# Hybrid attention encoder on one core: superblocks walked back and forth, keys of the next head group made for the current superblock, maxima taken through DRAM

## The chip, the cores and the metric

The kernel runs on one NeuronCore of a Trainium2 chip. TensorE (PE) multiplies, VectorE (DVE) and ScalarE (ACT) work elementwise, GpSimd (POOL) does small elementwise work, SyncE (SP) issues every DMA of this kernel. The metric is device time in microseconds, from one launch.

## The reference, cut to what matters

One layer is applied to two requests with the same weights: a prompt of 2048 rows and a sample of 512 rows, 1024 wide.

```python
h = rmsnorm(x, g_pre) * (1.0 + scale) + shift        # scale, shift, gate from silu(c) @ w_ada + b_ada
qa, ka, va, ga, qb, kb, vb, gb = split(h @ w_in)
# A: 8 heads of 64, three dilated windows (128,1), (512,4), (2048,16), mixed by their softmax denominators
ya = dilated_mixture(rope(qa), rope(ka), va) * silu(ga)
# B: 4 heads of 2 x 64 queries and keys, 128 values, dense over all rows
a  = softmax(q1 @ k1.T / 8) - lam * softmax(q2 @ k2.T / 8)
yb = rmsnorm(a @ v, g_sub) * (1.0 - lam_init) * silu(gb)
y  = concat(ya, yb) @ w_out
out = x + gate * rmsnorm(y, g_post)
```

## The kernel before

**Tiles.** A superblock is 512 rows of a request: the prompt has four (here p0 to p3), the sample one (s). The heads are cut into eight groups of 128 columns each of queries, gates, keys and values; groups 4 to 7 are dense attention (B), groups 0 to 3 dilated attention (A), and they are worked in the order 4, 0, 5, 1, 6, 2, 7, 3, so B and A alternate. Every f16 operand is held as a high and a low half, and a projection is three products (L433), so that the result has nearly f32 precision.

**Stages.** The first part, ahead of the group loop, makes the modulation, the normalised input h of each superblock (`first_h`, `make_h`), spills h to DRAM (`spill_h`, 2 MB for a superblock) and projects the first group. Then comes a double loop, group by group and superblock by superblock (L1036 to L1092), 40 stages in all. A stage's main work is the attention of one superblock in one group: 4 items of 128 queries in B, 8 items (2 heads by 4 blocks) in A. Its filler, woven between, is projection work for later stages: `qg_proj` of the next superblock (L523: queries, transposed by DMA into the tile Qc at L550, then 24 products for the gate), and `kv_proj` of the *next* superblock for the *next* group (L448). In the fifth stage the filler is both projections of p0 for the next group. The next stage's first scores (L602 in B, L711 in A) read Qc.

**h.** Two buffers in SBUF hold h of two superblocks (`HB`). `load_h` (L368) brings one back from DRAM as four DMAs of 512 KB; it is called once before the loop and then at the start of nearly every stage, 39 times.

**What sets the order.** The program is recorded with `interleave` (L963), which lets the filler run as far as the main work has come, against costs noted in the code, and with `LEAD` all zero. A scheduler then orders each engine's instructions by its own estimate of when they can run; each engine runs its list in order. In the group loop PSUM holds three buffers of scores, one of projections (`pj`) and one of outputs (`pv`, L1034).

**Maxima over all partitions.** Every weight group is scaled by a power of two from its largest element. `raw_scale` (L286) and `wo_scale` (L823) take it for w_in and w_out, `y_scale` (L874) for each superblock's y. All call `allmax`: a PE transpose of one column into a `pv` buffer, a DVE maximum over 128 numbers, and a PE product that spreads it to all partitions:

```python
tp = PT([P, 512], tag)
nc.tensor.transpose(tp[0:1, 0:P], col, id_sb)        # L178
m = T(tn, [1, 1], F32, "am1")
V.reduce_max(m, tp[0:1, 0:P], axis=AX.X)             # L180
bc = PT([P, 512], tag)
mm(bc[:, 0:1], lhsT=one_sb, rhs=m, start=True, stop=True)   # L182
```

**Output projection.** `out_proj` (L898) makes 20 tiles of 128 rows, 48 products each (L918), in part as filler of the last group, the rest after it. A tile begins with `y_first` (L885), which loads y from DRAM, and for a superblock's first tile calls `y_scale` before that.

Of the kernel before, what the change touches and what calls it, by code (L numbers as in the profile page):

```python
# [29 lines left out]
AQ = 1  # L30
LEAD = [0, 0, 0, 0]
OPC = [0, 20, 24, 24, 30]
# [5 lines left out]
def hybrid_kernel(ctx, tc, x_p, x_s, w_in, w_ada, w_out, cvec, cols, lamv, gsub,  # L38
# [136 lines left out]
    def allmax(col, tag="pv"):  # L175
# [7 lines left out]
        return bc[:, 0:1]  # L183

    RAW = {}

# [99 lines left out]
    def raw_scale(n):  # L286

        g, raw = ORDER[n], RAW[n]
        mg = T(tn, [P, 8], F32, "mg")
        for q in range(KT):  # L290
            V.tensor_reduce(mg[:, q:q + 1], raw[:, q, :], axis=AX.X, op=ALU.max, apply_absolute_value=True)
            yield 0.0
        ag = T(tn, [P, 1], F32, "ag")
        V.reduce_max(ag, mg, axis=AX.X)
        E = T(tn, [P, 1], F32, "E")
        S = C([P, 1], F32, f"wS{g}")
        pow2(E, S, allmax(ag), f"w{g}")
        smul(isw[:, g:g + 1], E, 2.0 ** -13)
        smul(S, S, 2.0 ** 12)
        WS[n] = S  # L300
        yield 0.0
# [107 lines left out]

    def first_h(r):  # L410

        for _ in norm_x(r, 0):
            pass
        xs = XN[r, 0]
        xT = [T(kv, [P, 4, 512], F32, "V") for _ in range(2)]
# [7 lines left out]
        hT = T(big, [P, 2, KT, 512], F16, "h", bufs=HB)  # L423
        HT[r, 0] = hT
        for k in range(KT):
# [3 lines left out]
            V.tensor_sub(hT[:, 1, k, :], xk, hT[:, 0, k, :])  # L429
        spill_h(r, 0)  # L430
        yield
# [391 lines left out]
    def wo_scale():  # L823
# [12 lines left out]
        wo["i"] = C([P, 1], F32, "woi")  # L836
        pow2(E, wo["S"], allmax(ag), "wo")
        smul(wo["i"], E, 2.0 ** -13 * 2.0 ** -13)
# [35 lines left out]
    def y_scale(r, c):  # L874

        ag = T(tn, [P, 1], F32, "ag")
        V.reduce_max(ag, yam[:, c + (r == "s") * NSB["p"], :], axis=AX.X)
        s = T(tn, [P, 4], F32, "ys")
        pow2(s[:, 0:1], s[:, 1:2], allmax(ag), "y")
        V.tensor_scalar(s[:, 0:1], s[:, 0:1], wo["i"], None, op0=ALU.mult)  # L880
        smul(s[:, 1:2], s[:, 1:2], 2.0 ** 12)
        V.tensor_scalar(s[:, 2:3], s[:, 0:1], s[:, 0:1], 1.0 / D, op0=ALU.mult, op1=ALU.mult)
        YS[r, c] = s

    def y_first(r, c, j):  # L885

        if j == 0:
            y_scale(r, c)
        s = YS[r, c]
# [92 lines left out]
    NS = len(SBS)  # L982
    outp = out_proj([(r, c, j) for r, c in SBS for j in range(4)])

# [10 lines left out]
    g0 = ORDER[0]  # L995
    h0 = first_h("p")
    next(h0)
# [19 lines left out]
    raw_load(1)  # L1017
    prev = ("p", 0)
    for n, (r, c) in enumerate(SBS):
        work = [kv_proj(r, g0, c)]  # L1020
        if n == 0:
            work.append(qg_proj(r, g0, c))
        if n == 2:
# [3 lines left out]
        if n + 1 < NS:  # L1027
            interleave(make_h(*SBS[n + 1]), 6.4, chain(*work), 11 * len(work))
        else:
            run(chain(*work))  # L1030
    if g0 < 4:
        load_v1("p", g0, 0)
    load_h(*SBS[1])
    psum(1024, 3, 1, 1)  # L1034

    for n, g in enumerate(ORDER):  # L1036
        if n + 1 == NU and g < 4:
            psum(1024, 2, 3, 1)
        g2 = ORDER[n + 1] if n + 1 < NU else None
        for i, (r, c) in enumerate(SBS):  # L1040
            fl, fc = [], 0.01
            side = iter(())
            if n + 1 < NU or i + 2 < NS:
                load_h(*SBS[(i + 2) % NS])
            if i == 0 and n + 2 < NU:
# [8 lines left out]
            elif n + 2 == NU:  # L1054
                if i < 2:
                    side = gate_half(i)
                elif i == 2:
                    side = wo_scale()
                elif i == 3:
                    side = load_wo(0)  # L1060
            elif i == 0:
                side = chain(load_wo(1), call(load_gg))
            if i == 0:
                at_n[3] = 0
            if i == 0 and g2 is not None:
                for x in "ps":
                    new_unit(x, g2)
            r2, c2 = SBS[(i + 1) % NS]
            if i + 1 < NS:
                fl.append(qg_proj(r2, g, c2))  # L1070
                fc += 11
                if g < 4:
                    fl.append(call(load_v1, r2, g, c2))
            if g2 is not None:
                fl.append(kv_proj(r2, g2, c2))
                fc += 11
                if i + 1 == NS:
                    for x in "ps":
                        fl.insert(0, call(unit_scalars, x, g2))
                    fl.append(qg_proj(r2, g2, c2))  # L1080
                    fc += 11
                    if g2 < 4:
                        fl.append(call(load_v1, r2, g2, c2))
            if g2 is None and i >= 1:
# [99 lines left out]
```

## Time and profile before

| what | us |
|---|---|
| median of 3 runs | 2179.29 |
| lowest, highest | 2177.16, 2189.58 |
| profiled execution | 2191.28 |
| its span, first to last instruction | 2189.5 |
| PE busy in the span | 1910.8 |
| DVE busy in the span | 1541.1 |
| ACT busy in the span | 1152.7 |

The profile is one execution, and its own time is 12.0 us above the median. A busy PE in it is the union of its matmuls. SyncE's work is DMA issues, which the page does not count as busy; each issue has a duration in the trace all the same.

### The profile page before, as it was taken

To read this page: it belongs to the slowest core of one execution; us is meant where nothing else is said; L and a number is where in the kernel's file an instruction comes from. 1 tells how busy PE (TensorE), PEld (TensorE's weight loads), DVE (VectorE), ACT (ScalarE), POOL (GpSimd) and SP (SyncE) were. 2 spreads that over 40 slices of the span, in tenths; PEclk is the share of its full clock that TensorE was granted. 3 is DMA by queue.
4 is the path that set the end of the run, shared out by engine and by line. 5 is a ranking of instruction groups with operands and counts; after the bars stand their busy time and mean duration, and the time that the engine had idled before them with its cause. 6 is when DMAs were issued, how large, how long until landed. Compare 5 with 4: busy or idle time off the path is not lost. (4 is left out here: it accounts for less than half of the span.)

```text
span 2189.5 us, 47689 instructions
## 1 busy us (share of the span) xinstructions
PE 1910.8 (87%) x18545; PEld 1285.2 (59%) x18545; DVE 1541.1 (70%) x3428; ACT 1152.7 (53%) x2278; POOL 394.9 (18%) x1049
## 2 busy tenths in 40 slices
PE   4878997898989988888899888897989878989898
PEld 2665665666767666666566666574665554444443
DVE  3777998676669988666599886666888665455543
ACT  3555665555547666555467665554566644333321
POOL 0122222221112222111122221111222121100000
PEclk7789999999999999999999999898999888999999
DMA  7585787888857789898477888888776779665553
GB/s 293 171 253 126 138 163 149 188 158 165 186 130 152 145 196 188 140 173 192 114 151 145 184 188 155 170 183 235 147 148 157 159 163 191 122 133 126 130 163 111
DMA packets 726834, 360.12 MB, mean 164 GB/s; under 512 B 639808, under 2 KB 686672, under 8 KB 723152
## 3 DMA queue, kind: packets, MB, share of 16 engines
q1 hardware_dynamic: 726608, 357.08, 73.6%
q8 instruction: 145, 2.38, 0.5%
q14 instruction: 81, 0.66, 0.1%
HBM read 164.79 MB, written 36.97 MB: 92 GB/s over the span
## 5 line engine op out<-in xcount | busy, mean ns | idle before, releaser
L460 PE MATMUL pj<-w,h 128*128 128x256 f16 x3840 | 480.9, 281 | 29.1 <-DVE V L476 8.2
L460 PEld LDWEIGHTS <-h 128*128 128x128 f16 x3840 | 379.1, 101 | 103.9 <-issue 40.5
L618 ACT ACTIVATE pp<-sc,nb 128x1024 f32<-128x1024 f32 (+1 forms) x288 | 304.3, 1060 | 100.2 <-DVE sc L611 83.2
L534 PE MATMUL pj<-w,h 128*128 128x128 f16 x3840 | 257.1, 223 | 15.0 <-ACT q L541 8.5
L534 PEld LDWEIGHTS <-h 128*128 128x128 f16 x3840 | 231.6, 100 | 43.4 <-issue 32.5
L557 PE MATMUL pj<-h,w 128*128 128x512 f16 x960 | 230.7, 392 | 17.9 <-ACT q L541 17.9
L656 PE MATMUL pv<-V,at 128*128 128x128 f16 x3072 | 207.5, 227 | 38.1 <-DVE yt L681 29.0
L656 PEld LDWEIGHTS <-at 128*128 128x128 f16 x3264 | 201.9, 102 | 64.6 <-issue 47.8
L747 DVE SCALAR_TENSOR_TENSOR hl<-pp,Z,hl 128x640 f16<-128x640 f32 (+2 forms) x160 | 140.3, 881 | 119.4 <-DMA at<-hl 71.6
L443 POOL TENSOR_TENSOR rp<-q,tab_sb 128x64 f32<-128x64 f32 x160 | 67.3, 420 | 788.4 <-ACT q L466 469.5
L745 ACT ACTIVATE hl<-pp,Z 128x640 f16<-128x640 f32 (+2 forms) x160 | 130.3, 823 | 132.5 <-DMA at<-hl 108.7
L611 DVE TENSOR_SCALAR_CACHE_REDUCE sc<-sc,us,nb 128x1024 f32<-128x1024 f32 x128 | 172.3, 1346 | 37.1 <-PE sc L608 15.9
L611 DVE TENSOR_SCALAR_CACHE_REDUCE sc<-sc,us 128x1024 f32<-128x1024 f32 (+1 forms) x160 | 188.1, 1179 | 10.8 <-PE sc L608 10.2
L636 ACT ACTIVATE hl<-pp,rz 128x1024 f16<-128x1024 f32 (+1 forms) x144 | 155.6, 1095 | 60.7 <-issue 38.7
L731 ACT ACTIVATE pp<-pp,nb 128x640 f32<-128x640 f32 (+2 forms) x160 | 131.5, 822 | 105.9 <-DVE nb L726 100.1
L644 DVE SCALAR_TENSOR_TENSOR hl<-pp,rz,hl 128x1024 f16<-128x1024 f32 (+1 forms) x144 | 174.5, 1223 | 16.8 <-DMA at<-hl 5.9
L602 PE MATMUL sc<-K,Qc 128*128 128x512 f16 x512 | 158.6, 389 | 30.2 <-ACT pp L618 29.5
L557 PEld LDWEIGHTS <-w 128*128 128x128 f16 x960 | 94.1, 100 | 135.6 <-issue 42.0
L634 DVE SCALAR_TENSOR_TENSOR pp<-pp,rz,pp 128x1024 f32<-128x1024 f32 (+1 forms) x144 | 171.2, 1225 | 1.9
L918 PEld LDWEIGHTS <-w 128*128 128x128 f16 x960 | 92.9, 99 | 125.0 <-issue 17.0
L711 PE MATMUL sc<-K,Qc 128*32 128x512 f16 (+1 forms) x1024 | 119.2, 371 | 27.0 <-DMA Qc<-tq 17.1
L724 DVE CUSTOM_DVE_ANT_0 pp<-sc,maskp,us 128x384 f32<-128x384 f32 (+1 forms) x128 | 85.8, 678 | 71.0 <-PE sc L717 70.8
(200 smaller groups left out, 2843.9 us busy)
## 6 DMA issues: line engine op xcount, KB each, us to landing
h<-hp SPq DMA_DIRECT2D x124, 512.0 KB, 6.0
pp<-in_x_p_dram SPq DMA_DIRECT2D x32, 512.0 KB, 5.0
raw<-in_w_in_dram SPq DMA_DIRECT2D x8, 2048.0 KB, 8.1
h<-hs SPq DMA_DIRECT2D x32, 512.0 KB, 5.7
out_dram<-pp SPq DMA_DIRECT2D x20, 512.0 KB, 2.9
at<-hl SPq DMA_TRANSPOSE x608, 3.2
hp<-h SPq DMA_DIRECT2D x4, 2048.0 KB, 9.3
yp<-yt SPq DMA_DIRECT2D x32, 256.0 KB, 3.2
```

The lines of the kernel that those rows point to most:

```text
L460: mm(ps[:, jj, :], lhsT=hT[:, a, k, j * P:(j + 1) * P], rhs=w[:, k, b, :], start=(k == 0 and i == 0), stop=(k == KT - 1 and i == 2))
L534: mm(ps[:, jj, 0:128], lhsT=hT[:, a, k, j * P:(j + 1) * P], rhs=w[:, k, b, 0:128], start=(k == 0 and i == 0), stop=(k == KT - 1 and i == 2))
L557: mm(ps, lhsT=w[:, k, b, 128:256], rhs=hT[:, a, k, :], start=(k == 0 and i == 0), stop=(k == KT - 1 and i == 2))
L602: mm(ps[:, n * 512:(n + 1) * 512], lhsT=Qc[:, j, m, 0, :], rhs=K[:, t:t + 4, m, :], start=True, stop=False)
L611: V.tensor_scalar(ps[:, :HW], ps[:, :HW], u["nsc"], nb[:, 0:1] if hf else 3e38, op0=ALU.mult, op1=ALU.min, accum_out=nb[:, hf:hf + 1])
L618: act(pt[m, hf][:, :HW], pss[hf][:, :HW], AF.Exp, scale=-1.0, bias=nb[:, NH - 1:NH], accum_out=Z[:, 2 * m + hf:2 * m + hf + 1])
L634: V.scalar_tensor_tensor(a, a, rz[:, 2:3], pt[0, hf][:, :HW], op0=ALU.mult, op1=ALU.add)
L636: act(hi[:, :HW], a, AF.Copy, scale=rz[:, 3:4])
L644: V.scalar_tensor_tensor(lo[:, :HW], a, sg, hi, op0=ALU.mult, op1=ALU.subtract)
L656: mm(po[:, :128], lhsT=a[:, k, :], rhs=Vv[:, k, 128 * b:128 * b + 128], start=(k == 0 and i == 0), stop=(k == NT - 1 and i == 2))
L731: act(sb[:, :NA], sb[:, :NA], AF.Exp, scale=-1.0, bias=nb[:, 1:2], accum_out=Z[:, 0:1])
L747: V.scalar_tensor_tensor(lo[:, :NA], sb[:, :NA], rz, hi[:, :NA], op0=ALU.mult, op1=ALU.subtract)
```

## The change

1. The sample's superblock goes to the middle: p0, p1, s, p2, p3. Groups at even places of the order walk that list forwards, those at odd places backwards, so a group begins with the superblock on which the one before ended.
2. The filler of a stage is now `kv_proj` of the *current* superblock for the next group, then `load_h` of the superblock two places on (if the group has one), then `load_v1` and `qg_proj` of the next superblock. In a group's last stage, `qg_proj` is of the same superblock for the next group. `load_h` is called 24 times.
3. Before the loop h is made from p3 to p0, and the first `qg_proj` stands at the end instead of beside the second superblock's `make_h`.
4. `LEAD` is replaced by a lead of 0.1 of the main work's cost.
5. All later maxima (`raw_scale` from the second group on, `wo_scale`, `y_scale`), 13 in number, go through `allmax_slow`: write the column to DRAM, read it back to every partition, DVE maximum over 128 numbers in each.
6. `y_scale` is called as soon as the eighth group's y of a superblock is written (in `y_out`), not when its first output tile begins. `gate_half`, `wo_scale` and the first `load_wo` are one stage later.

```diff
+    def allmax_slow(col):
+        d = dr.tile([P, 1], F32, tag=nm("amd"), name=nm("amd"))
+        nc.sync.dma_start(d, col)
+        row = T(tn, [P, P], F32, "amr", bufs=2)
+        nc.sync.dma_start(row, d.rearrange("p o -> (p o)").partition_broadcast(P))
+        m = T(tn, [P, 1], F32, "amc", bufs=2)
+        V.reduce_max(m, row, axis=AX.X)
+        return m
...
-        pow2(E, S, allmax(ag), f"w{g}")
+        pow2(E, S, (allmax if n == 0 else allmax_slow)(ag), f"w{g}")
...
         y_made[r, c] = y_made.get((r, c), 0) + 1
+        if y_made[r, c] == NU:
+            y_scale(r, c)
...
+    SBS.insert(NSB["p"] // 2, SBS.pop())
+    WAY = [SBS[::1 - 2 * (n % 2)] for n in range(NU)]
+    outp = out_proj([(r, c, j) for r, c in WAY[-1] for j in range(4)])
...
-            if n + 1 < NU or i + 2 < NS:
-                load_h(*SBS[(i + 2) % NS])
...
-            r2, c2 = SBS[(i + 1) % NS]
-            if i + 1 < NS:
-                fl.append(qg_proj(r2, g, c2))
-                fc += 11
-                if g < 4:
-                    fl.append(call(load_v1, r2, g, c2))
-            if g2 is not None:
-                fl.append(kv_proj(r2, g2, c2))
+            if g2 is not None:
+                fl.append(kv_proj(r, g2, c))
                 fc += 11
+            if i + 2 < NS:
+                fl.append(call(load_h, *way[i + 2]))
+            r2, c2, gq = (*way[i + 1], g) if i + 1 < NS else (r, c, g2)
+            if gq is not None:
...
+                if gq < 4:
+                    fl.append(call(load_v1, r2, gq, c2))
+                fl.append(qg_proj(r2, gq, c2))
                 fc += 11
...
-            interleave(main, mc, weave(chain(*fl), side), fc, LEAD[2 * (r == "p") + (g < 4)])
+            interleave(main, mc, weave(chain(*fl), side), fc, -AHEAD * mc)
```

What the scheduler made of it shows at three places. In the rows below weight loads and repeats are left out; the numbers behind names only keep buffers apart. Lines of the changed kernel are 10 to 12 higher: its L544, L567, L614, L620, L668, L723, L777 are L534, L557, L602, L608, L656, L711, L765 of before.

PE, the second group (A), where the dense group before it ends. Before: the last queries of p0 (`pj_5252`, 20 products without a break), 24 gate products, the first scores with its Qc.

```order
L656 MATMUL pv_5086<-Vs_454,at 128x128
...
L534 MATMUL pj_5252<-w_1573,h_3974 128x128
...
L557 MATMUL pj_5328<-h_3974,w_1573 128x512
...
L677 MATMUL pv_5164<-id_sb,o_5129 128x128
...
L711 MATMUL sc_5372<-K_1782,Qc_5111 32x384
```

The same place in the changed kernel, where the group begins with p3: last queries (`pj_5181`), 48 value products, scores of the dense group's last item, gate, scores.

```order
L544 MATMUL pj_5181<-w_1420,h_3479 128x128
...
L668 MATMUL pv_4812<-V_443,at 128x128
...
L620 MATMUL sc_4937<-K_442,Qc_4314 128x512
...
L567 MATMUL pj_5243<-h_3479,w_1420 128x512
...
L614 MATMUL sc_5104<-K_442,Qc_4314 128x512
...
L723 MATMUL sc_5277<-K_1772,Qc_5090 32x384
```

Between the last query product and the first score that reads it stood the gate alone; now 48 value products and 16 score products stand there too.

PE, the fourth group (A), at the start of a middle stage. Before, p3 to s: behind the 24 gate products (`pj_14368`) 32 score products of p3 stand ahead of the first that reads the new Qc (`Qc_14167`).

```order
L557 MATMUL pj_14368<-h_13501,w_7969 128x512
...
L711 MATMUL sc_14670<-K_8586,Qc_13515 32x384
...
L717 MATMUL sc_14670<-K_8586,Qc_13515 32x256
...
L711 MATMUL sc_14713<-K_8586,Qc_13515 32x384
...
L717 MATMUL sc_14713<-K_8586,Qc_13515 32x256
...
L711 MATMUL sc_14793<-Ks_8590,Qc_14167 32x128
```

The changed kernel, p3 to p2: behind the last query (`pj_12444`) and the 24 gate products (`pj_12557`) stands one value product, then the first score with the new Qc (`Qc_12353`).

```order
L544 MATMUL pj_12444<-w_7902,h_9833 128x128
...
L567 MATMUL pj_12557<-h_9833,w_7902 128x512
...
L777 MATMUL pv_12915<-at,V_8543 128x128
...
L723 MATMUL sc_12806<-K_8540,Qc_12353 32x512
```

What stood between the gate and the new scores is gone there.

The weight maximum in the second group. Before, on PE in the third group's p1 stage: transpose, key and value products, scores, spreading product.

```order
L608 MATMUL sc_9777<-K_5368,Qc_8602 128x512
L178 MATMUL pv_9675<-id_sb,ag_9671 1x128
...
L460 MATMUL pj_9979<-w_6687,h_8579 128x256
...
L608 MATMUL sc_9783<-K_5368,Qc_8602 128x512
L182 MATMUL pv_9679<-am_1475_9677,one_sb 128x1
```

The same maximum in the changed kernel, on SP: `amd` is the DRAM column, `amr` its copy in every partition.

```order
L761 DMA_TRANSPOSE at<-hl_8194 128x5x128
L188 DMA amd_9462<-ag_9458 128x1
L494 DMA_TRANSPOSE K_5273<-tk_8150 128x4x128
L583 DMA yp_117<-yt_7796 128x512
L190 DMA amr_9464<-amd_9462 128x128
L760 DMA_TRANSPOSE at<-hl_8247 128x5x128
```

Both PE instructions are gone; SP's list has two more issues, the second of which reads what the first wrote.

## Rows read from the trace of the kernel before

**Rows 1.** The page: busy time and share by engine, and 40 slices.
```profile
PE 1910.8 (87%) x18545; PEld 1285.2 (59%) x18545; DVE 1541.1 (70%) x3428; ACT 1152.7 (53%) x2278; POOL 394.9 (18%) x1049
PEclk7789999999999999999999999898999888999999
```

**Rows 2.** Windows (length; PE, PEld, DVE, ACT, POOL busy; clock): start, groups 3, 4, 7.
```profile
0.00:171.30 171.30, 123.06 (x917) 93.64 (x918) 99.52 (x260) 80.31 (x146) 31.47 (x81) 0.81 0.69 236
...
629.10:866.60 237.50, 218.26 (x2167) 150.21 (x2168) 210.84 (x362) 152.70 (x302) 57.79 (x146) 0.98 0.78 163
866.60:1070.40 203.80, 174.48 (x2153) 130.58 (x2153) 129.79 (x408) 106.14 (x215) 31.51 (x98) 0.95 0.82 162
...
1508.00:1790.20 282.20, 238.39 (x2227) 160.36 (x2227) 225.98 (x393) 164.00 (x324) 61.77 (x153) 0.92 0.76 167
```

**Rows 3.** SP's issues by line: duration ns (min/median/max), first and last start.
```profile
L748 SPq DMA_TRANSPOSE at<-hl x160: 1177/1234/3210, 441.1 to 2072.1; - x160
L550 SPq DMA_TRANSPOSE Qc<-tq x80: 1231/1254/2327, 91.7 to 1971.0; - x80
L371 SPq DMA_DIRECT2D h<-hp x124: 326/430/2009, 151.2 to 1827.3; - x124
```

**Rows 4.** PE's waits: who for whom, us in total, times, longest.
```profile
PE sc L711 <- DMA Qc<-tq: 24.1, 12, 5.0
...
PE pv L178 <- DVE ag L294: 10.6, 2, 9.6
...
PE pv L178 <- DVE yt L780: 4.4, 2, 2.4
...
PE pj L534 <- DMA h<-hp: 3.1, 1, 3.1
PE pv L182 <- DVE am L180: 3.0, 3, 1.4
PE pv L178 <- DVE ag L877: 3.0, 1, 3.0
```

**Rows 5.** Timeline of PE around the first output tile (start, length, idle before).
```profile
1844.76 0.37 PE L178 MATMUL pv<-id_sb,ag 128*1 128x128 f32 x1 [2.98 <-DVE ag L877]
...
1855.66 1.03 PE L918 MATMUL pj<-raw,w 128*128 128x512 f16 x2 [6.07 <-ACT w L894]
```

**Rows 6.** Window over the same place.
```profile
1841.80:1858.50 16.70, 6.48 (x42) 2.66 (x43) 9.60 (x26) 5.45 (x8) 0.00 (x0) 0.59 1.06 232
```

**Rows 7.** DMA issues: count, KB each, us to landing.
```profile
h<-hp SPq DMA_DIRECT2D x124, 512.0 KB, 6.0
...
h<-hs SPq DMA_DIRECT2D x32, 512.0 KB, 5.7
...
V<-vbp SPq DMA_DIRECT2D x64, 80.0 KB, 2.5
...
gg<-hl SPq DMA_DIRECT2D x1, 8.0 KB, 1.3
```

**Rows 8.** Windows of last stages (s): fourth, third and seventh group.
```profile
1010.70:1070.40 59.70, 47.38 (x554) 37.12 (x545) 34.18 (x111) 25.92 (x56) 7.90 (x28) 0.91 0.74 152
...
838.00:866.60 28.60, 23.77 (x240) 15.55 (x241) 18.66 (x42) 14.11 (x34) 8.18 (x22) 0.88 0.95 177
...
1743.60:1790.20 46.60, 30.91 (x317) 23.90 (x317) 30.99 (x73) 25.07 (x59) 13.36 (x33) 0.89 0.72 147
```

**Rows 9.** Timeline of PE where the seventh group ends.
```profile
1790.16 1.68 PE L711 MATMUL sc<-K,Qc 128*32 128x384 f16 x10 [5.01 <-DMA Qc<-tq]
```

**Rows 10.** Timeline of PE, fourth group, p3 to s.
```profile
1004.64 5.35 PE L557 MATMUL pj<-h,w 128*128 128x512 f16 x24
...
1014.07 0.29 PE L711 MATMUL sc<-Ks,Qc 128*32 128x128 f16 x6 [3.05 <-DMA Qc<-tq]
```

**Rows 11.** Timeline of SP over the same stretch.
```profile
1007.35 1.23 SPq L748 DMA_TRANSPOSE at<-hl  x1
1008.67 1.23 SPq L749 DMA_TRANSPOSE at<-hl  x1
1010.00 1.26 SPq L550 DMA_TRANSPOSE Qc<-tq  x1
```

**Rows 12.** Timeline of ACT there: the copy of the last queries, then L547.
```profile
1003.55 0.38 ACT L541 ACTIVATE q<-pj 128x256 f32<-128x256 f32 x1
...
1005.19 0.63 ACT L547 ACTIVATE tq<-q 128x512 f16<-128x512 f32 x1 [0.15 <-POOL q L446]
```

More of the change, by code (lines that the diff above doesn't have):

```diff
@@ L30 @@
 AQ = 1
-LEAD = [0, 0, 0, 0]
+AHEAD = 0.1
 OPC = [0, 20, 24, 24, 30]
@@ L408, in make_h, with first_h @@
         spill_h(r, c)
-    def first_h(r):
-        for _ in norm_x(r, 0):
+    def first_h(r, c):
+        for _ in norm_x(r, c):
             pass
-        xs = XN[r, 0]
+        xs = XN[r, c]
         xT = [T(kv, [P, 4, 512], F32, "V") for _ in range(2)]
@@ L423, in first_h @@
         hT = T(big, [P, 2, KT, 512], F16, "h", bufs=HB)
-        HT[r, 0] = hT
+        HT[r, c] = hT
         for k in range(KT):
@@ L429, in first_h @@
             V.tensor_sub(hT[:, 1, k, :], xk, hT[:, 0, k, :])
-        spill_h(r, 0)
+        spill_h(r, c)
         yield
@@ L877, in y_scale @@
         V.reduce_max(ag, yam[:, c + (r == "s") * NSB["p"], :], axis=AX.X)
-        s = T(tn, [P, 4], F32, "ys")
-        pow2(s[:, 0:1], s[:, 1:2], allmax(ag), "y")
+        s = T(tn, [P, 4], F32, "ys", bufs=5)
+        pow2(s[:, 0:1], s[:, 1:2], allmax_slow(ag), "y")
         V.tensor_scalar(s[:, 0:1], s[:, 0:1], wo["i"], None, op0=ALU.mult)
@@ L982, in hybrid_kernel @@
     NS = len(SBS)
-    outp = out_proj([(r, c, j) for r, c in SBS for j in range(4)])
+    SBS.insert(NSB["p"] // 2, SBS.pop())
+    WAY = [SBS[::1 - 2 * (n % 2)] for n in range(NU)]
+    outp = out_proj([(r, c, j) for r, c in WAY[-1] for j in range(4)])
     def upto(gen, cost):
@@ L995, in hybrid_kernel @@
     g0 = ORDER[0]
-    h0 = first_h("p")
+    h0 = first_h(*SBS[-1])
     next(h0)
@@ L1017, in hybrid_kernel @@
     raw_load(1)
-    prev = ("p", 0)
-    for n, (r, c) in enumerate(SBS):
+    for n, (r, c) in enumerate(SBS[::-1]):
         work = [kv_proj(r, g0, c)]
-        if n == 0:
-            work.append(qg_proj(r, g0, c))
         if n == 2:
@@ L1027, in hybrid_kernel @@
         if n + 1 < NS:
-            interleave(make_h(*SBS[n + 1]), 6.4, chain(*work), 11 * len(work))
+            interleave(make_h(*SBS[-2 - n]), 6.4, chain(*work), 11 * len(work))
         else:
-            run(chain(*work))
+            run(chain(*work, qg_proj(r, g0, c)))
     if g0 < 4:
-        load_v1("p", g0, 0)
-    load_h(*SBS[1])
+        load_v1(*SBS[0][:1], g0, SBS[0][1])
     psum(1024, 3, 1, 1)
@@ L1039, in hybrid_kernel @@
         g2 = ORDER[n + 1] if n + 1 < NU else None
-        for i, (r, c) in enumerate(SBS):
+        way = WAY[n]
+        for i, (r, c) in enumerate(way):
             fl, fc = [], 0.01
             side = iter(())
-            if n + 1 < NU or i + 2 < NS:
-                load_h(*SBS[(i + 2) % NS])
             if i == 0 and n + 2 < NU:
@@ L1054, in hybrid_kernel @@
             elif n + 2 == NU:
-                if i < 2:
-                    side = gate_half(i)
-                elif i == 2:
+                if 1 <= i < 3:
+                    side = gate_half(i - 1)
+                elif i == 3:
                     side = wo_scale()
-                elif i == 3:
+                elif i == 4:
                     side = load_wo(0)
```

12 lines of the change are left out of this document (3 added, 9 removed).

## The prediction

> **What bounds the kernel now.** I read the page first: PE is busy 87% of the span, far above the others, and its granted clock is below full in most slices [rows 1]. So PE's own work is the floor, and what can be won is PE's idle time (2189.5 - 1910.8 = 279 us) and what the lower clock adds. The change removes almost no PE work, so the question is which of PE's waits go and which come.
>
> Then the windows by stage of the program [rows 2]. The start is the worst stretch: 48 us idle of 171, clock 0.81. A dense group (the third) has PE idle 19 us of 237.5, with DVE busy 211: there PE and DVE are both near their limit. A dilated group (the fourth) has PE idle 29 us of 203.8 with DVE at 130, so DVE is not its limit. One transposing issue holds SP 1.23 us, whatever its tile [rows 3]. A dilated group issues 80 of them for its weights (4 and 1 superblocks of 8 items, high and low), 10 for its queries and 10 for the next group's keys: 100 x 1.23 = 123 us of SP, before plain DMAs. SP's list is therefore long in the very groups in which PE idles most, and a transfer that PE needs stands behind others there. Last, PE's waits by cause [rows 4]: the largest that this change can touch is the one for Qc, 24.1 us in 12 times, all in dilated groups.
>
> **Part by part.** The sum is made against the profiled execution, 2191.3 us.
>
> *Maxima off PE.* 13 of 16 go. The waits in front of L178 and L182 are 10.6 + 4.4 + 3.0 + 3.0 us [rows 4], but 9.6 of the first is one wait, which I take as that of the first weight group, which keeps its maximum on PE. 11.4 us go. Around the first output tile PE also stands 6.07 us for the tile's scaled y, behind that chain [rows 5]; with the scale made earlier I take half of it, 3 us. That stretch of 16.7 us has a clock of 0.59 and 6.5 us of PE work [rows 6]; at full clock about half of that work's time is saved, 3 us. Gain: 17 us.
>
> *The price of the way through DRAM.* Two issues and the landing of the first, for which SP must wait before it issues the second, with everything behind it in its list held: weight transposes, Qc, the next h. The trace has no such pair. The nearest single rows: a small write to DRAM lands 1.3 us after issue, an 80 KB load after 2.5 [rows 7]. SP held: between 0 (the order puts other ready issues between the two) and 13 x 2.5 = 33 us. In the order shown two issues stand between them, in others none. I take 1.3 us in four of the thirteen, 5 us: the write is nearest in size to the one added, and the weight groups' maxima fall in dense stages as often as in dilated ones. The DVE maximum (128 numbers in every partition) I cost at nothing, since results are wanted a stage later; in the last group it has the remaining output tiles as cover.
>
> The Trainium skill, page "DMA: Bandwidth & Descriptors", section "Two DMAs through the same engine are not ordered", says that a DMA which reads what another wrote must be issued only after the first one's completion has reached the issuing engine; its section on the anatomy of a DMA puts that completion at some 2 us, the more so when the target is DRAM. By that page the hold would be 13 x 2 = 26 us as an estimate; the write in [rows 7] landed in 1.3. It speaks against this part of the change, as the slower rival below does by rows alone.
>
> *Loads of h.* 24 calls for 39, so 60 issues fewer, 60 x 0.43 = 26 us of SP's time [rows 3], about what the thirteen pairs may cost it: I set the two against each other as far as the list's length goes. PE waited for h once, 3.1 us [rows 4]; after the start the first two superblocks are already in SBUF, so that goes. That transposes land sooner with 31 MB fewer in flight I leave at nothing, since the loads are hidden. Bounds: 0 and 10 us gained. Taken: 3.
>
> *Ends of groups.* A dilated group now ends with a prompt superblock. The old last stage (the sample) has PE idle 59.7 - 47.4 = 12.3 us [rows 8], the other four of that group (29.3 - 12.3) / 4 = 4.3 [rows 2]. Three such ends at 8 us too many make 24; I take half, 12, since the sample's stage has to stand somewhere, though now without the next group's keys to finish. A dense group ended with the sample too: 4.8 us idle at one end, 15.7 at the worst [rows 8], and there the next scores waited 5.0 us for Qc [rows 9]. Now 48 value and 16 score products stand in that place. I take 8 us for the four. The clock in these stretches is 0.88 to 0.91 against 0.95 to 0.98 for whole groups [rows 2, 8]: 0.04 of three times 47 us of work, and a little for the dense ends, 7 us. Bounds: 0 (the wait moves into the middle) and 40. Taken: 27.
>
> *The projections' order.* Before, the queries for the next superblock came first and the keys behind them; now the keys come first and the queries last. In dense stages this costs nothing that I can see: the first item needs only the first half of Qc, and scores of the running superblock cover it. In dilated groups the row to read is p3 to s of the fourth [rows 10 to 12]: ACT takes the last queries at 1003.55, SP issues Qc at 1010.00 behind two weight transposes, and PE goes on at 1014.07: 10.5 us. The gate covers 5.35, other scores the remaining 2.1, and 3.05 is idle. In the changed order the first scores of p2 and of p1 in the second, fourth and sixth group have the gate and at most nine products before them, 6.0 us at most: 10.5 - 6.0 = 4.5 us idle, six times, 27 us. Before, 24.1 us fell on 12 waits, ends of groups among them, so I take 8 us for the same six places. Loss: 19. Bounds: 0 (if Qc is issued when its tile is ready, some 6 us after the last query) and 45 (if it waits behind two more transposes each time).
>
> *The rest.* The lead of 0.1 and the new start (queries last, with no h being made beside them) have no row. The nearest is the start's 48 us of idle [rows 2]; a third of it either way, -15 to +15. Taken: 0, since the products are the same and both orders fill the same waits.
>
> Sum: -17 + 5 - 3 - 27 + 19 = -23, so 2168 us for a run like the profiled one. That one stands 12 us above the median, 0.55%; scaled to it, 2179.3 x 2168 / 2191.3 = 2156.
>
> **The rivals.** *Nothing measurable.* Each kind of group has a second engine near its limit, DVE in dense groups (211 of 237.5 us), SP's list in dilated ones, and neither list gets shorter; a PE wait removed is given back as the next wait for the same engine. For it: [rows 2, 3]. Against it: the waits at L178 are PE's own, and the ends of groups idle on both engines. Only the waits at L178 and L182 would stay gained, and the query loss and the DRAM price take that back: 2175 to 2185, say 2180.
>
> *Slower, by Qc behind SP's list.* The queries are the last filler of every stage, SP holds back its list for the maxima, and Qc, the last transfer that PE needs, lands last. The price is the upper end of the query term, 45, with 20 for the held list, against gains cut to 17, 3 and 15: +30, 2210. It decides from about 8 us idle at each of the six starts. For it: 10.5 us from the last query to the scores in [rows 10 to 12], of which SP's queue is a large part. Against it: the scheduler put other products into the gap at p0 and s.
>
> *Much faster, because the two kinds of group overlap.* If dense tails (DVE) run beside dilated starts (SP), dilated groups idle no more than dense ones: 29 to 19 us, three times 10, and clock 0.95 to 0.98 of 204, three times 6. That is 48 more: -71, 2109. For it: the 48 value products that now stand in the next group's first stage. Against it: nothing shortens a group's own lists. The Trainium skill, page "Perfetto Trace Analysis", section "Optimization Strategy", names this mechanism: where regimes have different busiest engines, interleave them. The trace shows the two regimes; no run here shows the interleaving.
>
> **How the numbers follow.** Forecast 0.47, nothing 0.23, slower 0.20, much faster 0.10. The likeliest time is 2156, its own range 2130 to 2175 from the bounds above (loss 0 to 30, ends 12 to 35). The whole range takes in most of the slower case and all but the best of the faster: 2105 to 2208. About 0.5%, 11 us, is what a measurement of this kernel can tell from no change. Faster than 2168: 0.42 of the forecast, all of the much faster, 0.04 of the second, 0.56. Slower than 2190: 0.17 of the third, 0.03 of the second, 0.01 of the first, 0.21. The rest is 0.23.
>
> **What would show it.** Right: no PE wait at L178 after the start; idle at group ends down to 4 to 8 us a stage; waits of the scores L723 for Qc up from 24 to some 40 us, mostly in p2 and p1 of dilated groups; DMA volume down by 31 MB. Wrong: waits for Qc of 60 us or more, or waits of Qc's issue for the DRAM column; or a start that is 15 us longer; or group spans of 237 and 204 us as before, with PE's idle time only renamed.

## The result, and the profile after

The changed kernel takes 2324.57 us (median of 4 runs, 2317.09 to 2327.14), the one before 2182.18 beside it: a ratio of 1.0644, 95% interval 1.0601 to 1.0687, so 140 us slower (131 to 150). The forecast was 23 us faster. The slower rival had the right sign with 30 us, but, as will be seen, not the mechanism.

The page of the changed kernel, against [rows 1]: PE is 55 us longer busy for the same work.

```profile
PE 1966.1 (85%) x18506; PEld 1293.9 (56%) x18506; DVE 1543.6 (66%) x3428; ACT 1151.8 (50%) x2278; POOL 393.8 (17%) x1049
...
PEclk7899999999999989999899988999898987899999
```

Windows of the same stretches as [rows 2], start and third, fourth and seventh group, in their columns; then the fourth group's first stage (p3) and its last (p0), and the third's last (p3), which answer to [rows 8].

```profile
0.00:180.90 180.90, 122.59 (x914) 92.18 (x915) 102.21 (x271) 82.40 (x150) 31.79 (x81) 0.85 0.60 213
640.00:898.50 258.50, 224.19 (x2123) 150.53 (x2121) 211.73 (x375) 154.02 (x310) 61.10 (x150) 0.95 0.65 130
898.50:1122.00 223.50, 188.09 (x2229) 141.33 (x2228) 133.06 (x398) 105.03 (x209) 30.95 (x94) 0.94 0.67 137
1595.80:1900.50 304.70, 244.50 (x2271) 168.65 (x2267) 222.17 (x399) 166.97 (x333) 62.31 (x160) 0.91 0.70 150
898.50:951.90 53.40, 42.48 (x536) 33.60 (x536) 31.06 (x91) 25.37 (x54) 9.82 (x26) 0.92 0.76 159
1073.90:1122.00 48.10, 37.65 (x433) 31.23 (x433) 34.21 (x93) 23.66 (x45) 5.35 (x18) 0.82 0.61 127
832.70:898.50 65.80, 48.16 (x411) 29.97 (x408) 53.74 (x93) 36.53 (x71) 13.44 (x32) 0.88 0.49 109
```

The loss is spread: the start is 10 us longer, and the three groups shown 21, 20 and 23 us. Only the first group, measured in the same way, got shorter, 238 us for 257, and the second longer by as much, 221 for 200; from the third on every group is longer.

Waits in the changed kernel, by PE, DVE and SP, in the columns of [rows 4].

```profile
PE sc L614 <- ACT pp L630: 53.3, 32, 8.8
PE pv L668 <- DMA at<-hl: 37.7, 22, 4.1
PE pv L777 <- DMA at<-hl: 37.1, 20, 5.1
...
PE pj L928 <- ACT w L904: 23.8, 1, 23.8
...
PE sc L723 <- DMA Qc<-tq: 10.1, 10, 2.2
...
DVE amc L192 <- DMA amr<-amd: 109.5, 13, 18.8
...
SPq L190 <- DMA amd<-ag: 74.6, 12, 7.4
```

Qc is waited for less than before (24.1 in [rows 4]), where the forecast had 40. What is new: DVE stands 109.5 us for the thirteen rows of maxima, SP 74.6 us in 12 waits for the columns, and PE waits 74.8 us for the transposed weights `at` (21.3 before). By source line, the two transfers of a maximum (the pair, below): the column (0.5 KB, 128 runs of 4 bytes) and the row:

```profile
L188 SPq DMA_DIRECT2D amd<-ag x13: 320/381/609, 72.0 to 2219.7; - x13
...
DMA to landing us min/median/max: 6.8/7.6/9.4
```

```profile
L190 SPq DMA_DIRECT2D amr<-amd x13: 319/325/541, 79.1 to 2226.9; - x13
...
DMA to landing us min/median/max: 3.1/4.7/7.8
```

The first output tile, where PE had waited 6.07 us [rows 5], in the timelines of DVE, SP and PE:

```profile
1962.15 0.16 DVE L889 TENSOR_REDUCE ag<-yam 128x1 f32<-128x8 f32 x1
1981.10 0.29 DVE L192 TENSOR_REDUCE amc<-amr 128x1 f32<-128x128 f32 x1 [18.78 <-DMA amr<-amd]
...
1964.92 0.38 SPq L188 DMA_DIRECT2D amd<-ag  x1
...
1973.32 0.33 SPq L190 DMA_DIRECT2D amr<-amd  x1
...
1983.49 1.04 PE L928 MATMUL pj<-raw,w 128*128 128x512 f16 x2 [23.81 <-ACT w L904]
```

DVE has the maximum next in its list and does nothing for 18.78 us, and PE stands 23.81. One view more of this stretch, the DMA engines between the column's issue and its landing (40 equal slices, GB/s in each, then the issues with their time to landing):

```profile
GB/s 206 41 279 366 405 185 1 193 39 135 116 154 116 96 154 39 19 0 0 0 39 19 19 0 58 0 19 58 58 19 39 0 0 19 19 19 39 0 39 0
...
h<-hp SPq DMA_DIRECT2D x2, 512.0 KB, 12.2
...
amd<-ag SPq DMA_DIRECT2D x1, 0.5 KB, 8.3
```

The two loads of h issued right behind the column, 1 MB, land after 12.2 us (6.0 in [rows 7]), and from the 17th slice on, 5 us, the core moves 58 GB/s at most. The trace's records of single DMA packets say what is slow. The packets of 4 bytes, the column's among them, took 7 to 9 ns each and were through by 1966.4, though the column landed at 1973.3. The packets of 4 KB behind it, of the loads of h, took 1.56 us each by the median up to 1974, and 6.2 at most; over the whole run their median is 0.159. This is the sight that the experiments come back to.

### The profile page after: what moved, and what is told of

Its sections match the earlier page's. It is cut to its first block, busy times and chain, and to the rows that moved or that the text cites. A ratio compares the mean times of both kernels' runs of the same rounds, so it can differ in the third digit from the quotient of the medians.

```text
span 2325.3 us, 47563 instructions
## 1 busy us (share of the span) xinstructions
PE 1966.1 (85%) x18506; PEld 1293.9 (56%) x18506; DVE 1543.6 (66%) x3428; ACT 1151.8 (50%) x2278; POOL 393.8 (17%) x1049
## 2 busy tenths in 40 slices
DMA packets 721939, 329.53 MB, mean 142 GB/s; under 512 B 640928, under 2 KB 689456, under 8 KB 718256
## 5 line engine op out<-in xcount | busy, mean ns | idle before, releaser
L470 PE MATMUL pj<-w,h 128*128 128x256 f16 x3840 | 498.4, 282 | 59.2 <-DVE V L486 20.2
L544 PE MATMUL pj<-w,h 128*128 128x128 f16 x3840 | 253.8, 225 | 28.0 <-DVE V L486 12.6
L544 PEld LDWEIGHTS <-h 128*128 128x128 f16 x3840 | 232.2, 101 | 53.6 <-issue 42.4
L567 PE MATMUL pj<-h,w 128*128 128x512 f16 x960 | 239.0, 397 | 24.7 <-ACT q L551 24.7
L668 PE MATMUL pv<-V,at 128*128 128x128 f16 x3072 | 207.8, 227 | 45.6 <-DMA at<-hl 34.8
L668 PEld LDWEIGHTS <-at 128*128 128x128 f16 x3264 | 202.4, 102 | 72.4 <-DMA at<-hl 44.6
L453 POOL TENSOR_TENSOR rp<-q,tab_sb 128x64 f32<-128x64 f32 x160 | 73.1, 457 | 861.9 <-ACT q L476 529.6
L614 PE MATMUL sc<-K,Qc 128*128 128x512 f16 x512 | 160.4, 392 | 51.2 <-ACT pp L630 51.2
L656 DVE SCALAR_TENSOR_TENSOR hl<-pp,rz,hl 128x1024 f16<-128x1024 f32 (+1 forms) x144 | 175.3, 1223 | 30.9 <-DMA at<-hl 17.7
L567 PEld LDWEIGHTS <-w 128*128 128x128 f16 x960 | 95.2, 102 | 143.5 <-issue 53.5
L723 PE MATMUL sc<-K,Qc 128*32 128x512 f16 (+1 forms) x1024 | 128.8, 369 | 19.6 <-DMA Qc<-tq 10.1
L928 PE MATMUL pj<-raw,w 128*128 128x512 f16 x480 | 122.2, 386 | 23.8 <-ACT w L904 23.8
```

The lines of the kernel that those rows point to most:

```text
L470: mm(ps[:, jj, :], lhsT=hT[:, a, k, j * P:(j + 1) * P], rhs=w[:, k, b, :], start=(k == 0 and i == 0), stop=(k == KT - 1 and i == 2))
L544: mm(ps[:, jj, 0:128], lhsT=hT[:, a, k, j * P:(j + 1) * P], rhs=w[:, k, b, 0:128], start=(k == 0 and i == 0), stop=(k == KT - 1 and i == 2))
L567: mm(ps, lhsT=w[:, k, b, 128:256], rhs=hT[:, a, k, :], start=(k == 0 and i == 0), stop=(k == KT - 1 and i == 2))
L614: mm(ps[:, n * 512:(n + 1) * 512], lhsT=Qc[:, j, m, 0, :], rhs=K[:, t:t + 4, m, :], start=True, stop=False)
L656: V.scalar_tensor_tensor(lo[:, :HW], a, sg, hi, op0=ALU.mult, op1=ALU.subtract)
L668: mm(po[:, :128], lhsT=a[:, k, :], rhs=Vv[:, k, 128 * b:128 * b + 128], start=(k == 0 and i == 0), stop=(k == NT - 1 and i == 2))
```

## The experiments

Times are given as what the kernel takes over before, by the ratio to runs of before beside it, with the 95% interval of the ratio. The change itself is at +140.

### Which half: e1 and e2

e1 is the change with every maximum on PE; e2 is before with the maxima by DRAM alone.

```diff
 e1 (on after):  -pow2(E, S, (allmax if n == 0 else allmax_slow)(ag), ...)   +pow2(E, S, allmax(ag), ...)   (also wo, y)
 e2 (on before): -pow2(E, S, allmax(ag), ...)   +pow2(E, S, (allmax if n == 0 else allmax_slow)(ag), ...)   (also wo, y)
```

> The changed kernel with its thirteen maxima back on PE (allmax); walk, projections' order, lead and early y scale stay. Theory 1 (DVE stands in its list at the maximum over the DRAM copy, 109.5 us in 13 waits, and SP 74.6 us at the copy's issue, and PE starves behind them): most of the 142 us go, 2180 to 2225. Rival (the new order of projections and superblocks makes the loss): it stays above 2280.

> The kernel before, with the thirteen maxima through DRAM and nothing else changed. Theory 1: 2182 plus 90 to 130, so 2270 to 2310, with DVE waits at the maximum of about 110 us in 13 times. Rival (order): 2170 to 2200, since the waits would be taken up by slack that the kernel before has.

e1: +79 us (70 to 87). e2: +101 (93 to 109). e2 came out as theory 1 had it, but neither theory has all: DRAM costs about 100 us alone and 62 in the change (140 - 79), and the changed order costs 79 without it. Two windows of e1, the fourth group's first stage (p3) and last (p0), and the same group's first stage (p0) before:

```profile
880.40:928.20 47.80, 34.58 (x438) 25.80 (x437) 30.63 (x90) 23.78 (x50) 7.76 (x23) 0.86 0.74 163
1053.10:1089.80 36.70, 32.92 (x434) 27.12 (x434) 30.04 (x82) 20.51 (x40) 5.56 (x18) 0.95 0.63 144
```

```profile
866.60:886.00 19.40, 18.47 (x277) 12.86 (x276) 18.18 (x69) 14.74 (x36) 5.21 (x16) 1.00 1.00 189
```

PE's idle time at the group's end went from 12.3 us [rows 8] to 3.8, as forecast (in the change itself to 48.10 - 37.65 = 10.4); at its beginning it went from 0.9 to 13.2, in a stage that now has keys and queries to make and no old scores beside them. Taken whole, though, the dilated group is the lesser loss. The third group (dense) and the fourth (dilated) of e1, against 237.50 and 203.80 us in [rows 2]:

```profile
624.00:880.40 256.40, 231.90 (x2225) 159.06 (x2224) 213.66 (x377) 156.83 (x314) 59.25 (x153) 0.97 0.66 133
880.40:1089.80 209.40, 178.33 (x2136) 132.36 (x2136) 133.17 (x396) 103.50 (x205) 27.64 (x91) 0.93 0.68 142
```

The dense one is 19 us longer, with 58 more products in it, the dilated one 6. The fifth group (254.7 for 235.6) and the sixth (210.2 for 202.0) say the same.

### When the row is read, and writes without a reader: e3 and e5

e3 is the change with DVE's maximum written in the code where its result is used; e5 is before with 28 small writes to DRAM that nobody waits for.

```diff
 e3 (on after):  -V.reduce_max(m, row, axis=AX.X)   +def rest(): V.reduce_max(m, row, axis=AX.X) ...   (called in raw_split, load_wo, y_first)
 e5 (on before): +nc.sync.dma_start(dr.tile([rows, cols], F32, ...), raw[0:rows, q, 0:cols])   (1x128, 128x128, 128x16, 128x1)
```

> The changed kernel, but the maximum over the DRAM copy and what follows on DVE stand where the scale is first used (the split of the weights one stage later, the first output tile of a superblock), not behind the DMA. SP's two issues stay as they are. If DVE's wait is the cost: its waits at the maximum fall from 109.5 to under 45 us (the eight for weights mostly gone, some for y left), and the time by 60 to 100, to 2225 to 2265. If SP's held list (74.6 us) is the cost: the time falls by less than 40, above 2285.

> The kernel before with 28 more writes to DRAM for which nothing waits: in each of seven weight groups one of 1 x 128 numbers (512 bytes in one row), 128 x 128, 128 x 16 and 128 x 1. If the 4-byte rows make the landing slow, 128 x 1 lands in 7 us and 128 x 128 in under 4; if 128 separate rows do, all three of these land in about 7 us and the single row in 1 to 2. Either way theory 1 says the time stays within 0.7% of before, since no list waits for a landing; the rival of a write that clogs the DMA engines says 2200 or more.

e3: +148 (139 to 157), no better than the change; the scheduler put the maximum at the same place of DVE's list, so this says nothing on DVE's wait. e5: +7 (2 to 12). Transposes issued behind its writes landed after up to 9.8 us (in before, too, the slowest take 9.4), and PE's waits for `at` rose from 21 to 51 us in sum, yet little time was lost; I took it for proof that writes are harmless, which was too early. Its question, 4-byte runs or 128 runs, stays open: the landings that the trace can tell are 7.5 and 9.8 us for 128 x 1, and 1.5 and 8.6 for 128 x 16.

### The order part: f1 to f4, f8

All but f8 stand on e1 (+79); f8 is before with the lead of 0.1 alone.

```diff
 f1: -AHEAD = 0.1   +AHEAD = 0
 f2: fl = [qg_proj(next, g), kv_proj(current, g2), load_h(way[i + 2])]      (e1: keys, load, queries)
 f3: -WAY = [SBS[::1 - 2 * (n % 2)] for n in range(NU)]   +WAY = [SBS for n in range(NU)]   (h loaded as before)
 f4: -nc.sync.dma_start(u["vb"]..., Vt)   +nc.gpsimd.dma_start(u["vb"]..., Vt)
 f8: -interleave(..., LEAD[...])   +interleave(..., -0.1 * mc)
```

> Base: the change with every maximum on PE, 77 us slower than before. Here the lead of 0.1 is 0 as before, all else of the change's order stays. Theory 'lead' (filler placed a tenth of a stage earlier takes PE from the scores that feed DVE, so the dense groups stretch): 30 to 60 us come back, 2200 to 2225, and the dense groups n2 and n4 drop from 255 towards 240 us. Theory 'keys first' (the price is the order of the projections and SP held by V): 0 to 10 us, 2245 to 2260.

> Base as for the run with the lead at 0 (2257). Here the filler begins with the queries of the next superblock, as before, and the keys follow; walk, place of the sample, lead and loads of h stay as changed. Theory 'keys first': 40 to 77 us come back, 2180 to 2215, and the issue of the V write is waited for less than 40 us on SP (73 in the base). Theory 'lead' and theory 'walk': under 15 us come back, 2240 to 2260.

> Base 2257. Here every group walks the superblocks forwards (the sample still in the middle), h is loaded 39 times again; keys of the current superblock come first, as in the change. Theory 'walk' (on backward passes the first stage of a dilated group needs all of the last projected superblock's K and V at once and has the sparse start): 30 us or more come back, 2225 or less. Theory 'keys first' and theory 'lead': 2245 to 2275, or a little slower for 15 more loads of h.

> Base 2257. Here the 80 writes of V to DRAM for the dilated groups are issued on GpSimd's queue instead of SP's, so SP isn't held by them (73 us in 15 places in the base); all else stays. Theory 'SP held': 25 to 60 us come back, 2195 to 2230. If SP's hold is only the time in which nothing else was ready: under 10 us, 2245 to 2262; GpSimd's rope products may come late behind the writes, up to 10 us lost.

> The kernel before with the lead of 0.1 alone, all else as it was. Theory 'the lead takes PE's time from the scores in every order': 20 to 40 us slower than before, 2200 to 2220. Theory 'the lead costs only where the keys come first and the queries last' (with queries first it gave back nothing): within 8 us of before.

f1 +48 (41 to 54): the lead is 31 of the 79. f2 +53 (45 to 61): the queries' place is about 25. f3 +80 (72 to 89) and f4 +76 (71 to 82; 40 writes of V in its trace): neither the walk nor SP's hold by V is a cause. f8 +10 (6 to 14): in the order of before the lead costs 10, with the keys first 31.

### Queries first: f6 and f7

f6 is f2 with the lead at 0. f7 is f6 with the queries of a group's later superblocks computed from the current superblock's h, so that they wait for no load (the loads stay; the output is not the reference's).

```diff
 f6: -AHEAD = 0.1   +AHEAD = 0
 f7: -fl.append(qg_proj(r2, g, c2))   +fl.append(qg_proj(r2, g, c2, HT[r, c]))
```

> Base: the change with every maximum on PE, queries first and lead 0.1 (2239 us, of which PE waited 57 us for h). Here the lead is 0 as well. The lead alone gave back 31 us with the keys first. Theory 'two prices that add': 2200 to 2215. Theory 'h held by the keys' (the keys of the current superblock keep its h buffer until late in the stage, so the h of the superblock after next is loaded late): waits of the queries' products L544 for h stay at 40 us or grow, and so the time stays at 2205 to 2235. If the two prices were one and the same: 2235 to 2245.

> As the run with queries first and lead 0, but the queries and gates inside a group are computed from the h of the current superblock instead of the next one's (so the output is not the reference's; work and transfers are the same), so they never wait for the load of h. Theory 'h held by the keys': PE's waits at L544 for h vanish and the time falls by 20 to 55 us against that run, to 2150 to 2190. Rival (the h wait is only where other waits would stand): within 10 us of it.

f6 stays at +59 (53 to 65): with the queries first, lead or none, the price is the same. f7: +10 (6 to 14), so 49 us of f6 are one thing. PE's waits in f6 show it:

```profile
PE pj L544 <- DMA h<-hp: 43.1, 24, 5.1
PE pj L544 <- DMA h<-hs: 25.6, 14, 3.9
```

These 68.7 us are gone in f7. There are two buffers of h. The keys of the current superblock keep one until they are made, so the next h can only be loaded behind them. With queries first this makes h late. With keys first, as in the change, h comes in time (PE never waits for it), and the price, 48 us without the lead (f1), is not one wait. In e1 PE waits 46.7 us for `at` (21.3 before) and 14.3 for Qc (24.1 before), and the queries now wait for DVE's copy of the values that were made just before them in the one `pj` buffer; e1's line, and before's:

```profile
PE pj L544 <- DVE V L486: 17.2, 12, 3.8
```

```profile
PE pj L534 <- DVE V L476: 1.4, 3, 0.6
```

No run takes one of these waits away, so what the keys' place costs, and by which of them, is not shown. Before, keys and queries were both of the next superblock, and a buffer was free as the stage began.

### Late, or on another queue: g1 and g2

Both on e2 (+101). g1 gives the weights' maxima one more column, a zero made from an item of the next stage, so that they stand some 200 instructions later in DVE's list. g2 issues the thirteen pairs on GpSimd's queue.

```diff
 g1: +act(row[:, P:P + 1], LAST[0], AF.Copy, scale=0.0)      LAST[0]: a column of the item's hi
     -V.reduce_max(m, row, axis=AX.X)   (row now 129 wide, called at the first raw_split)
 g2: -nc.sync.dma_start(d, col)   +nc.gpsimd.dma_start(d, col)   (the read too)
```

> Base: before with the maxima by DRAM, 2281 us, 101 us over before. Here DVE's maximum over the row of a weight group (six of them, and w_out) takes one more column, a zero made from an item of the next stage, so that it stands some 200 instructions later in DVE's list; the two transfers stay where they were on SP; the five for y and the second weight group in the start stay as in the base. Theory 'DVE held in order': DVE's waits at that maximum fall from 120 to some 50 us, and 45 to 65 us come back: 2215 to 2235. Rival 'SP held for the first landing' (87 us): 0 to 15 us come back, 2265 to 2285.

> Base as for the late maximum (2281). Here both transfers of each of the thirteen pairs are issued on GpSimd's queue, so SP is never held by them (87 us in the base), while DVE still waits for the row. Theory 'DVE held in order': DVE's waits stay at 100 us or more and the time within 20 us of the base, 2260 to 2290. Rival 'SP held': 45 us or more come back, 2235 or less. GpSimd then is held itself, 7 to 9 us a time, and its rope and root products with it.

g1: +85 (77 to 93), though DVE's wait fell from 119.6 to

```profile
DVE amc L196 <- DMA amr<-amd: 52.4, 6, 16.8
```

so 67 us of waiting gave back 16. g2: +92 (86 to 98), not to be told from e2, with 78.9 us of DVE's waiting left. g1 speaks against DVE's wait as the price, g2 against SP's: neither theory holds for both. A column that g2 issues in the third group, issues and landings in a window of 14 us:

```profile
vbs<-Vs SPq DMA_DIRECT2D x1, 128.0 KB, 12.6
at<-hl SPq DMA_TRANSPOSE x4, 12.8
...
amd<-ag POOLq DMA_DIRECT2D x1, 0.5 KB, 13.9
```

The column is on GpSimd's queue, where SP does not wait for it, and still four transposes from SP's land after 12.8 us by their median (3.3 over the run). So it is not SP's waiting that makes them late, but what stands on the DMA engines.

### With like lists: c1, c2, c3, and d1

c1, c2 and c3 stand on e2. DVE takes its maximum over a constant row that is ready, so the scales are not the reference's. c1 keeps both transfers; in c2 the second reads a column written at the start, so that SP waits for none of the later ones; c3 has neither transfer. The order of the other instructions is the same in all three on every engine, but for a stretch of the last group. d1 is before with PE's maxima kept and the pairs and DVE's maxima added, their results unused.

```diff
 c1: -V.reduce_max(m, row, axis=AX.X)   +V.tensor_copy(own[:, P:P + 1], col); V.reduce_max(m, own, axis=AX.X)
 c2: c1, and -nc.sync.dma_start(row, d...)   +nc.sync.dma_start(row, D0[0]...)
 c3: c1 without both dma_start
 d1 (on before): +allmax_slow(ag)   ahead of each later allmax(ag)
```

> Base: before with the maxima by DRAM, 2281 us (+101). Here the column still goes to DRAM and back on SP, but DVE takes its maximum (128 numbers in each partition, at the same place) over a constant row that is ready, so that it never waits for the transfers (the scales are then other numbers than the reference's). Theory 'DVE held in order is the price': 70 us or more come back, 2185 to 2210. Theory 'SP held is the price': 0 to 30 come back, 2250 to 2280. Theory 'each hold is enough by itself, since what one engine holds back the other waits for anyway': about as much as the two runs before gave, 10 to 30 us, 2250 to 2270.

> As the run with the constant row, and the second transfer reads a column that was written at the start, so SP isn't held by the first landing either; the thirteen writes and reads remain, as do the thirteen DVE maxima. Theory 'the two holds are the price, whichever': 2175 to 2200. Rival 'the changed place of everything else in the lists is the price, as the scheduler laid the lists out anew': still 40 us or more above before, 2220 to 2280. The DVE and PE lists of this run and the run with the constant row are alike, so their difference is SP's hold alone.

> The run with the constant row once more, without any transfer of the maxima: neither PE's two steps nor the thirteen pairs are there, DVE takes its maximum over the constant row (scales other than the reference's). PE's and DVE's lists are as in the two runs that took the waits away. Theory 'the lists laid out anew are the price': still 60 us or more above before, 2240 to 2265. Theory 'the pair on SP is the price': within 15 us of before.

> The kernel before with every maximum on PE as it was, and the way through DRAM beside it: the thirteen pairs on SP and DVE's thirteen maxima over the rows, whose results nobody reads. PE keeps the instructions that the DRAM way had taken out. Theory 'the two waits are the price': 60 us or more over before, 2240 to 2285, with DVE waiting 80 us or more for the rows. Theory 'the lists without PE's own steps are the price, the waits some 15 to 20 us': 2190 to 2215.

c1 +77 (66 to 88), c2 +80 (71 to 90), c3 +19 (12 to 25), d1 +90 (84 to 96). Set against e2's 101, 19 come without any transfer, from lists that are laid out anew without PE's steps. From e2 to c1, without DVE's wait, 24 come back (101 - 77); as the lists of these two differ, that is only roughly what the wait is worth. Taking SP's wait away on top gives nothing in the sum. The remaining 60 come with the transfers, though behind the start of c2 no engine waits for one of them. c2 has a flaw: its reads all gather in the start, where SP waits 20.3 us for them, and the start takes 181.7 us (c1 165.8, c3 159.6 in their profiles). Outside the start c2 is thus some 40 us over c3 (80 - 19 - 22) and c1 some 52 (77 - 19 - 6), so SP's hold and the reads in their places may be worth a dozen; the runs spread too far to tell. The 40 are the columns' alone. d1, with both waits in it (DVE 122.4 us, SP 89.5), says the same from the other side: PE's steps can stay, the price comes with the transfers and their waits. Where PE loses it, its waits for `at` tell, in c2 and then in c3:

```profile
PE pv L671 <- DMA at<-hl: 51.9, 36, 7.7
PE pv L780 <- DMA at<-hl: 39.3, 25, 5.5
```

```profile
PE pv L666 <- DMA at<-hl: 42.9, 31, 3.1
PE pv L775 <- DMA at<-hl: 17.8, 15, 3.0
```

These are 91.2 us for 60.7: 30 of the 40. How, c2 shows behind a column in the first group (SP's timeline; then the 11 us from there, GB/s and landings):

```profile
380.12 0.53 SPq L188 DMA_DIRECT2D amd<-ag  x1
...
381.70 2.46 SPq L506 DMA_TRANSPOSE Ks<-tk  x2
384.25 7.84 SPq L652 DMA_TRANSPOSE at<-hl  x2
```

```profile
GB/s 281 280 288 187 294 134 305 357 332 285 198 137 13 9 0 130 72 2 0 6 1 4 1 3 0 3 1 0 0 2 0 0 4 6 9 6 40 66 137 248
...
vbs<-Vs SPq DMA_DIRECT2D x1, 128.0 KB, 11.6
at<-hl SPq DMA_TRANSPOSE x3, 7.4
...
amd<-ag SPq DMA_DIRECT2D x1, 0.5 KB, 10.4
```

From the 18th slice to the 36th, 5 us, the core moves less than 10 GB/s, with V, two transposes of keys and one of weights issued behind the column; V lands 2 us behind it. SP's next two transposes take 7.84 us to issue (1.23 each in [rows 3]). c3 at the same place, 10 us:

```profile
vbp<-V SPq DMA_DIRECT2D x1, 128.0 KB, 2.6
...
at<-hl SPq DMA_TRANSPOSE x4, 4.7
```

So here a column of 0.5 KB holds what is issued behind it until it has landed, 10.4 us. About 40 us for the eleven columns behind the start is 3.6 us each as a mean, but no fixed price: c2's second, third and fifth groups are 5 to 8 us longer than c3's and the last, with five columns, 16, while the first, with the column shown here, is 2 us longer.

The packet records set these runs apart from e5. A packet that takes more than 4 us is found only within 14 us behind such a column: 10 of them in the change, 43 in e2, 39 in c1, 51 in c2, 9 in d1, 66 in g2. There is none in before, e1 or c3, and none in e5, whose seven columns are of the same shape and whose longest packet takes 3.7 us. Why e5's columns hold nothing so long is not shown.

### The scale of y early: b1

b1 is before with `y_scale` called in `y_out`, by PE as before.

```diff
+        if y_made[r, c] == NU:
+            y_scale(r, c)
```

> The kernel before with one part of the change alone: the scale of y is made when the last group's y of a superblock is written, by PE as before. By the prediction's term for the first output tile (6.07 us of waiting, and a clock of 0.59 over 16.7 us) 3 to 6 us are gained: 2173 to 2180. If the wait only moves: within 2 us of before. It is the candidate for a version ahead of both.

+1 (-4 to +5): nothing. The first output product still waits:

```profile
1847.72 1.03 PE L918 MATMUL pj<-raw,w 128*128 128x512 f16 x2 [6.01 <-ACT w L894]
```

The scheduler gives this maximum the same place in DVE's list in both kernels, so the earlier call moved nothing. No version tried is ahead of the kernel before.

## Why the prediction was wrong

- *The price of the way through DRAM*, +5, is the step that failed most. I took 1.3 us from a write of 8 KB and charged it to SP, four times. Alone it measures 82 us (101 - 19): some 60 by the transfers, and roughly 24 by DVE's wait. "SP held" was the wrong account: SP's 85 us of waiting were worth a dozen at most (c1 against c2), and on GpSimd's queue the pairs cost as much (g2). The bytes were the wrong measure: the row taken was 16 runs of 512 bytes, the column is 128 runs of 4 bytes and lands after 6.8 to 9.4 us, and no row of before showed such a write. The range I gave it, 0 to 33, had no end for a transfer that holds others.
- "*The DVE maximum I cost at nothing, since results are wanted a stage later*": a result's late use does not make its instruction late. DVE's list has it next, for 109.5 us. Read late (g1), 67 us less of this wait gave 16.
- *Maxima off PE*, -17: PE's waits at L178 did go, all but the first group's (8.9 us). But c3, without them and without any transfer, is 19 us slower than before. A wait gone from PE's list brought another order of that list, not a gain. The early scale's share is nothing (b1).
- *Ends of groups*, -27: right at the dilated ends by size (12.3 us to 3.8 in the fourth, e1; 10.4 in the change), wrong in what it leaves: the idle time stands at the same group's beginning, 13.2 us for 0.9. I had named that bound, "the wait moves into the middle"; it moved to the start of the dilated group, where no stretch was priced. The dense ends gained nothing: in the change PE is idle 65.80 - 48.16 = 17.6 us in the third group's, 4.8 before.
- *The projections' order*, +19: the sign was right, the place wrong. Waits of L723 for Qc fell to 10.1 us. "In dense stages this costs nothing that I can see" failed: the third and fifth groups of e1 are 19 us longer each, the dilated ones 6 to 8. With queries first the price is that of the buffer of h (f6 against f7, 49 us); with keys first it is as large, and its cause is not shown. f1, f2 and f6 give 48 to 59 for either order without DRAM, where ends and queries together were -8.
- *The rest*, 0 (15 either way): the lead costs +10 alone (f8), 31 with the keys first (f1). The new start costs nothing, 169.1 us in e1 for 171.3; the change's 180.9 come with the two pairs in it.
- *Loads of h*, -3, and DMA volume down by 31 MB: the volume came true (360.12 MB to 329.53), PE waits for h no more, and neither shows in the time.

Of the rivals, *slower by Qc behind SP's list* had the held list, but its 20 us for it are a quarter of the 82 that the way through DRAM costs alone, and Qc was not what came late. *Much faster by overlap* did not show: dilated groups went from 204 to 223 us.

Not settled: why PE is 55 us longer busy with the same products in the change (44 in e1) at a clock of 0.93 to 0.95 for 0.94. The starts of the products say where. From one product's start to the next one's, without the idle time that the profile counts, pass 500 us in sum before where the next product is of another line of the kernel (2720 times), 558 in the change (2704) and 553 in e1 (2728); between products of one line the sum did not grow. So the time goes where one kind of work follows another, perhaps in short waits; no run here takes them away. Nor is it shown why e5's writes, some of them such columns, cost so little.

## What to carry to other kernels

Price a transfer by its shape and by what is queued behind it, not by its bytes: measure one of its shape with traffic behind it before the change counts on it. Ask of each piece of filler which buffer it keeps until when; "keys of the current superblock" was a change of a buffer's life, not of an order. To find a wait's worth, take it away with every list kept alike (c1 to c3): the sum of waiting that the profile shows, 120 us of DVE and 87 of SP in e2, was not what either was worth.

## What the runs showed of the hardware

A write of one column (128 partitions, 4 bytes each) to DRAM landed after 6.8 to 9.4 us in the change, and up to 13.9 us with other traffic (g2), for 8 KB in 16 runs of 512 bytes in 1.3 [rows 7]. The Trainium skill, page "DMA: Bandwidth & Descriptors", section "Specifications", says that below 512 bytes a transfer is handled by read-modify-write; its section on the anatomy of a DMA has some 2 us fixed cost, given there for GpSimd's path. By the second an estimate for the column is about 2 us; the trace has over three times that on SP's queue and more on GpSimd's, and the measurement decides. No run here shows whether read-modify-write is the reason. The other transfers' delay when the column is on GpSimd's queue (12.8 us for transposes of 3.3 by the median) agrees with the same page's section "Issuing engines are not separate DMA queues": all queues end on the same 16 engines, and another queue saves only the issuing time.
